# Expert weights stored four rows to a partition, and an earlier transpose of the next expert's rows

## Chip, cores and metric

One NeuronCore of a Trainium2 chip runs the whole program: two decoder layers over 1024 tokens. The metric is the device time in microseconds. Five engines work side by side, each through its own list of instructions in order: TensorE (PE; its weight loads are listed as PEld), VectorE (DVE), ScalarE (ACT), GpSimd (POOL) and SyncE (SP), which issues most of the transfers (DMA) between the chip's memory (DRAM) and the on-chip memory SBUF. TensorE writes its results to PSUM.

## The reference

Each of two layers adds two things to a stream of 1024 tokens by 1024 features: a mixer (eight heads of forgetting attention and eight of latent attention, then an output projection) and a mixture of experts. Only the second matters here. A token is normed, goes to one of 8 groups and to 2 of the 4 experts of its group, and an expert is a gated network of width 256:

```python
group_p = jax.nn.softmax((xt @ w_group).astype(jnp.float32), axis=-1)
group_w, group_id = lax.top_k(group_p, 1)
...
top_logits, local_id = lax.top_k(in_group, TOP_K_IN_GROUP)
gates = group_w * jax.nn.softmax(top_logits, axis=-1)
...
h = jax.nn.silu(xb @ w_gate[e]) * (xb @ w_up[e])
return h @ w_down[e]
...
y = jax.ops.segment_sum(contrib, tok_sorted, num_segments=T)
```

There are 32 experts in each layer. `w_gate` and `w_up` of one are 1024 x 256, `w_down` is 256 x 1024, all float32, 3 MB together. A last norm closes the program.

## The kernel before

**Arithmetic.** A matmul in full precision is done in three passes: each operand is split into a high part (ScalarE copies it into a shorter format, `hi`) and a low part (VectorE subtracts, `lo`), and `mm3` (lines 195 to 197) adds high x high, high x low and low x high. Activations are the stationary operand and the split weights the moving one.

**Experts.** Each expert has room for 96 rows (`RB`). `moe` (line 1541) runs a software pipeline over n = 0 to 32: in step n the current expert is n, the one before is n - 1 and the next is n + 1. All engines but SyncE take their instructions in the order in which the program lists them (`manual_schedule`, line 97). The stages of an expert are functions in `expert` (line 1426):

- `load_a` (1434) and `load_b` (1448): SyncE loads gate and up weights (`load_gu`, line 347, four transfers of 512 KB into two tiles) and down weights (one of 1 MB). Eight tiles hold gate and up weights of four experts; a load waits until the tile it overwrites has been split.
- `gather` (1458): GpSimd clears a tile and fetches the expert's rows from the stored norm `xn_d` by index, three steps ahead.
- `piece(j)` (1465): splits 128 x 1024 weights, on ScalarE (1468) and VectorE (1469). Pieces 0 to 3 are gate and up, each with two of the eight blocks of 128 features; 4 and 5 are down.
- `flip_x` (1473): eight transposes of the gathered rows on TensorE (1479), and a split of each half (185 on ScalarE, 186 on VectorE).
- `gate_up(q)` (1482): twelve matmuls of 512 columns for each half q; `silu` (1491); `flip_h` (1496): two transposes of the product and a split; `down` (1503): twelve matmuls; `result` (1512): two copies on ScalarE (1515, 1516) and a scatter on GpSimd.

**Order of a step.** Engines see, in this order:

```python
cur["gate_up"](0);  pieces_to(6 * n + PC[0])   # PC = (1, 4)
prev["flip_h"]();   cur["gate_up"](1)
prev["down"]();     pieces_to(6 * n + PC[1])
cur["silu"]();      prev["result"]()
nxt["flip_x"]();    pieces_to(6 * n + 6)
```

The pieces of step n are, by `ORDER` (line 53), (n,4), (n,5), (n+1,0), (n+1,1), (n+1,2), (n+1,3): one behind `gate_up(0)`, three behind `down`, two at the end of the step. `gate_up(0)` of an expert reads its pieces 0 and 1, `gate_up(1)` pieces 2 and 3.

**Layout of the weights.** Feature f of the model lies in partition f mod 128 of block f // 128. A gate or up transfer takes 512 rows of 256 floats: from DRAM each run is one row, 1 KB, and in SBUF gate and up alternate within a block, so that a block's 512 columns are gate beside up.

**The norm.** Ahead of the loop the output projection makes the residual tiles; `norm` (1095) squares, scales and stores each in `xn_d` (VectorE at 1103). The last of the eight tiles is done in halves on GpSimd (`norm_half`, 1118, line 1125), and `halves` (1109) splits the first expert's gate and up weights there, with GpSimd in VectorE's place (1113).

Of the kernel before, what the change touches and what calls it, by code (L numbers as in the profile page):

```python
# [20 lines left out]
P = 128  # L21
# [61 lines left out]
def kernel(ctx: ExitStack, tc: tile.TileContext, x, positions, attn_norm, w_in, b_f, q_norm, w_uq,  # L83
# [48 lines left out]
    # gains, one feature per partition  # L132
# [31 lines left out]
    def rsqrt(dst, v, n, tag, c=1.0):  # L164
        """dst = c * v ** -0.5, with a Newton step behind the engine's own power."""
        y = small.tile([P, n], F32, name="rs_y", tag=f"rs_y{tag}")
        pool.tensor_tensor(y, v, mhalf[:, 0:n], op=OP.pow)  # L167
        t = small.tile([P, n], F32, name="rs_t", tag=f"rs_t{tag}")
        pool.tensor_tensor(t, y, y, op=OP.mult)  # L169
        pool.tensor_tensor(t, t, v, op=OP.mult)  # L170
        pool.tensor_scalar(t, t, -0.5 * c, 1.5 * c, op0=OP.mult, op1=OP.add)  # L171
        pool.tensor_tensor(dst, y, t, op=OP.mult)  # L172
# [9 lines left out]
    def split(hi, lo, src, scale=None):  # L182
        """hi + lo = src * scale, each with as many bits as one pass of the tensor engine carries."""
        if scale is None:
            act.activation(hi, src, AF.Copy)  # L185
            dve.tensor_tensor(lo, src, hi.bitcast(F32), op=OP.subtract)  # L186
        else:
            act.activation(hi, src, AF.Copy, scale=scale)
            dve.scalar_tensor_tensor(lo, src, scale, hi.bitcast(F32), op0=OP.mult, op1=OP.subtract)

    def mm3(ps, sh, sl, mh, ml, kcs, first=True, last=True):
        """ps += s.T @ m over the chunks, three passes."""
        n = len(kcs)
        for i, kc in enumerate(kcs):
            pe.matmul(ps, sh(kc), mh(kc), start=first and i == 0, stop=False)  # L195
            pe.matmul(ps, sh(kc), ml(kc), start=False, stop=False)  # L196
            pe.matmul(ps, sl(kc), mh(kc), start=False, stop=last and i == n - 1)  # L197
# [15 lines left out]
    # DRAM kept between phases  # L213
# [5 lines left out]
    def combined(l, i, ht, y_):  # L219
        """The residual stream's tile behind layer l - 1."""  # L220
        if l == 0:
            return ht
        for j in range(2):
            y = y_(j)
            sp.dma_start(y, y_d[l - 1][j * T + i * P:j * T + (i + 1) * P])
            dve.scalar_tensor_tensor(ht, y, gates[:, j, i:i + 1], ht, op0=OP.mult, op1=OP.add)  # L226
        if l < DEPTH:
            sp.dma_start(h_d[2 * l - 1][i], ht)
        return ht
# [106 lines left out]
    def gu_tiles(p, tags=("mix", "mix"), more=None):  # L336
        r = []
        for t in tags:
            q = p
            if t == "mix":  # L340
                gu_n[0] += 1
                if GUX and gu_n[0] > 8 and gu_n[0] % 9 == 0 and more is not None:
                    q, t = more, "gux"
            r.append(q.tile([P, 4, 2 * FF], F32, name="gu", tag=t))
        return r

    def load_gu(raw, wg_, wu_):
        for q in range(2):
            ks = slice(q * 512, q * 512 + 512)
            sp.dma_start(raw[q][:, :, 0:FF], wg_[ks].rearrange("(k p) n -> p k n", p=P))  # L350
            sp.dma_start(raw[q][:, :, FF:], wu_[ks].rearrange("(k p) n -> p k n", p=P))
# [6 lines left out]
    def mixer_open(l):  # L358
        """What a layer can load before the one in front of it is through."""
        # room of the latents, which takes tiles of the residual stream first  # L360
# [17 lines left out]
    def mixer(l, opened):  # L378
        h_in = [xv[i] for i in range(NT)] if l == 0 else h_d[2 * l - 1]
        h_out = h_d[2 * l]  # L380
        # operands of a forgetting head as rows: q_hi twice, q_lo, 1, 1, c_hi, c_lo; k_lo, k_hi, -c_hi, -c_lo, 1, 1
# [123 lines left out]
        # ---- values, queries and keys of the forgetting heads; beside it what hangs on misc -  # L505
# [32 lines left out]
        def forget_a():  # L538
            # log_sigmoid(z) = min(z, 0) - log1p(exp(-|z|)); log1p by its series in u / (2 + u)
            z, u, s1, s2 = t_("fz"), t_("fu"), t_("fs"), t_("fs2")  # L540
            fl.update(z=z, u=u, s1=s1, s2=s2)
            dve.tensor_tensor(z, misc[:, :, 0:H], bft[:, l][:, None, :].to_broadcast([P, NT, H]), op=OP.add)
            dve.scalar_tensor_tensor(u, z, -1.0, z, op0=OP.mult, op1=OP.min)
            act.activation(u, u, AF.Exp)
# [17 lines left out]
        def forget_c():  # L562
            # sums within a token tile, and behind them those of the tiles before
# [82 lines left out]
        def v_scale(g, tp):  # L646
            # a power of two that puts the largest value between 2**14 and 2**15
# [28 lines left out]
        def late_pools():  # L676
            # where the values and misc were: weights of the latent projections, tables of the rotation
# [256 lines left out]
        def fin_a(h):  # L934
            # normed rows: y / sqrt(mean(y * y) + eps * Z * Z), with y and Z scaled alike
# [24 lines left out]
        def fin_c(p, half, bank=1):  # L960
            ysb = pairs[p][0].rearrange("p t s d -> p t (s d)")
            # the bank of the second head's results, which the next pair comes to use later
# [10 lines left out]
        # the output projection's weights, two blocks of rows to a piece, where attention has done  # L973
# [120 lines left out]

        def norm(i):
            ht = hts[i]
            sp.dma_start(h_out[i], ht)
            if i < NT - 1:
# [4 lines left out]
                dve.scalar_tensor_tensor(xn, ht, rs[:, i:i + 1], gb, op0=OP.mult, op1=OP.mult)  # L1103
# [5 lines left out]
        def halves(j):  # L1109
            hi, lo = hl[j]  # L1110
            raw = early[0][j // 2][:, j % 2 * 2:j % 2 * 2 + 2].rearrange("p k n -> p (k n)")
            act.activation(hi, raw, AF.Copy)
            pool.tensor_tensor(lo, raw, hi.bitcast(F32), op=OP.subtract)
# [3 lines left out]
        def norm_half(c):  # L1117
            """What the last tile's norm can do half by half."""
# [6 lines left out]
            pool.tensor_tensor(xn[:, cs], hts[NT - 1][:, cs], gb[:, cs], op=OP.mult)  # L1125
# [4 lines left out]
        # the router's operands are the tile before its norm: w_rt carries the gains, the gates' exponents the scales  # L1130
# [18 lines left out]
        def route_group(rg, a, b, lg=None):  # L1149
            """Experts, gates and ranks of the tokens of tiles a to b, and their entries in the blocks."""  # L1150
# [43 lines left out]
            # ranks within an expert by token; block NT holds the counts  # L1194
# [23 lines left out]
            # gates  # L1218
# [17 lines left out]
        # weights of the first experts, where attention's values and then its results have been  # L1236
        gu_n[0] = 0
        raw0 = v1.tile([P, 2, 4, 2 * FF], F32, name="V", tag="V")
# [11 lines left out]
        for i in range(NT):  # L1250
# [25 lines left out]
            if i == NT - 1:  # L1276
                # the first expert's gate and up weights in two parts, where those of w_o have been
# [35 lines left out]
        # rows of the blocks: which assignment sits where  # L1313
# [10 lines left out]
        # the experts' counts, and the number of further blocks they need  # L1324
# [7 lines left out]
        # behind the rows of the first experts  # L1332
# [13 lines left out]
    def more_tables(l):  # L1346
        """Blocks for the rows of an expert beyond the first RB: their experts, and which assignment sits where."""
# [28 lines left out]
        # of an assignment: the first further block of its expert, the block and the row its rank puts it in  # L1376
# [11 lines left out]
        # block of + qd - 1 where qd > 0, none elsewhere  # L1388
# [20 lines left out]
    def moe_open(l, v0, v1, mp, early, downs, dn_close, hl, hl_close, spare_close):  # L1409
# [16 lines left out]
        def expert(pools, wg_, wu_, wd_, gi, si, n=None):  # L1426
            """The stages of one block of rows, each to be issued where its engines have time."""
# [6 lines left out]
            def load_a():  # L1434
# [5 lines left out]
                e["raw"] = [raw[q][:, k:k + 2] for q in range(2) for k in (0, 2)]  # L1440
# [24 lines left out]
            def piece(j, eng=dve):  # L1465
                hi, lo = hl.popleft()
                raw = (e["raw"][j] if j < 4 else e["rawd"][j - 4]).rearrange("p k n -> p (k n)")
                act.activation(hi, raw, AF.Copy)  # L1468
                eng.tensor_tensor(lo, raw, hi.bitcast(F32), op=OP.subtract)  # L1469
# [12 lines left out]
            def gate_up(q):  # L1482
                if q == 0:
                    e["gu"] = ps_([RB, 2 * FF], F32, name="gu")
                at = lambda w: lambda k: w[k // 2][:, (k % 2) * 512:(k % 2) * 512 + 512]
# [55 lines left out]
    def moe(l, m):  # L1541
# [16 lines left out]
        for n in range(NE + 1):  # L1558
# [10 lines left out]
            if cur:  # L1569
                cur["gate_up"](1)  # L1570
            if prev:
# [6 lines left out]
            if l == DEPTH - 1 and n >= KEPT and len(kept) < NT:  # L1578
                # the weights are through: their room takes the residual stream for the last step
                for raw in gu_tiles(mp):  # L1580
                    for t in range(2):
                        kept.append(raw.rearrange("p k n -> p (k n)")[:, t * D:(t + 1) * D])
                        sp.dma_start(kept[-1], h_d[2 * l][len(kept) - 1])
            if nxt:
                nxt["flip_x"]()
# [103 lines left out]
```

## Time and profile before

| | us |
|---|---|
| median of three runs | 1997.6 |
| lowest and highest | 1996.01, 2002.56 |
| profiled execution, span from first to last instruction | 1997.8 |
| TensorE busy | 1760.9 (88%) |
| VectorE busy | 1347.5 (67%) |
| ScalarE busy | 1187.7 (59%) |
| GpSimd busy | 568.4 (28%) |

The page shows the span alone for the profiled execution and no time around it. It moved 427.11 MB in 243684 DMA packets, 146470 of them of 512 B to under 2 KB. In its slices of 50 us the DMA engines are full in two places, from about 650 to 950 us and from about 1600 to 1940 us: the expert loops of the two layers. A group's line gives the engine's busy time in it, the mean of one instruction, and how long the engine stood idle just before such instructions and whom it waited for. In a window's row the busy times stand in the order PE, PEld, DVE, ACT, POOL; a timeline row gives the start, how long, the engine, the line, output <- input with partitions x elements, how many were merged, and in brackets the idle time before and whom it waited for. A matmul's duration contains its way through the array; matmuls follow each other faster than they last.

### The profile page before, as it was taken

How to read it: one execution, taken by the hardware profiler on the slowest of the kernel's cores; microseconds unless marked ns; L12 is line 12 of the kernel's file. 1: busy time of each engine (PE TensorE's matmuls, PEld its weight loads, DVE VectorE, ACT ScalarE, POOL GpSimd, SP SyncE). 2: the span in 40 equal slices, each digit the busy share in tenths (PEclk: the TensorE clock that was granted, in tenths of full speed). 3: DMA queues.
4: the chain of work that ended last, by engine and by line, in shares of the span. 5: the costliest groups of instructions: out<-in, count | busy, mean ns of one | idle time of the engine just before them, and what ended most of it. 6: DMA issues, size and time to landing. Idle time of an engine off the chain costs nothing. (4 is left out here: it accounts for less than half of the span.)

```text
span 1997.8 us, 33752 instructions
## 1 busy us (share of the span) xinstructions
PE 1760.9 (88%) x12509; PEld 1420.1 (71%) x12509; DVE 1347.5 (67%) x2172; ACT 1187.7 (59%) x2254; POOL 568.4 (28%) x857
## 2 busy tenths in 40 slices
PE   7999899999995999998499997999999689998870
PEld 6987688888883666666399786888888556666650
DVE  6454388887246888877555355888852678887756
ACT  4443278788214888877344235888841278887751
POOL 4001044234114333331230021623330333332305
PEclk9999999999997999999799998999999889999995
DMA  4257833553755999999742775334455499999986
GB/s 157 64 126 218 261 119 108 114 123 96 251 185 180 345 333 333 327 325 331 284 137 54 203 242 183 126 101 109 114 196 209 148 297 324 327 332 322 321 295 235
DMA packets 243684, 427.11 MB, mean 214 GB/s; under 512 B 22166, under 2 KB 168636, under 8 KB 240444
## 3 DMA queue, kind: packets, MB, share of 16 engines
q1 hardware_dynamic: 228092, 387.14, 61.2%
q0 software_dynamic: 14336, 33.58, 5.2%
q10 hardware_dynamic: 1088, 4.19, 0.7%
q8 instruction: 100, 1.64, 0.3%
q14 instruction: 68, 0.56, 0.1%
HBM read 347.24 MB, written 94.37 MB: 221 GB/s over the span
## 5 line engine op out<-in xcount | busy, mean ns | idle before, releaser
L1469 DVE TENSOR_TENSOR lo<-gu,hi 128x1024 fp32r<-128x1024 f32 x248 | 292.6, 1222 | 41.6 <-ACT hi L1468 41.6
L1468 ACT ACTIVATE hi<-gu 128x1024 fp32r<-128x1024 f32 x248 | 248.4, 1054 | 26.4 <-DMA gu<-in_w_up_dram 20.5
L195 PE MATMUL gu<-hi,V 128*96 128x512 f32 x512 | 214.8, 420 | 38.4 <-ACT V L185 38.4
L885 PE MATMUL S<-op 96*128 96x512 f32 (+3 forms) x960 | 228.8, 372 | 20.2 <-DMA op<-FK 13.2
L897 DVE TENSOR_REDUCE nm<-S 128x1 f32<-128x1024 f32 (+7 forms) x256 | 183.2, 752 | 69.3 <-PE S L889 69.3
L906 ACT ACTIVATE pr<-S,nm 128x1024 f32<-128x1024 f32 (+7 forms) x256 | 188.9, 754 | 38.0 <-DVE nm L897 37.9
L197 PE MATMUL gu<-hi,V 128*96 128x512 f32 x512 | 210.0, 410 | 0.0
L196 PE MATMUL gu<-lo,V 128*96 128x512 f32 x512 | 205.7, 402 | 0.0
L916 ACT ACTIVATE ph<-pt 128x512 f16<-128x512 f32 x288 | 157.1, 600 | 66.8 <-PE pt L914 65.8
L917 DVE SCALAR_TENSOR_TENSOR pl<-pt,ph 128x512 f16<-128x512 f32 x288 | 184.7, 682 | 8.6 <-ACT ph L916 7.8
L885 PEld LDWEIGHTS S<-op 96*128 96x128 f32 (+1 forms) x960 | 161.5, 196 | 37.5 <-DMA wor<-in_w_o_dram 14.5
L1517 POOL DMA_INDIRECT y<-V,sidx x64 | 59.7, 932 | 441.6 <-ACT V L1516 417.4
L914 PE MATMUL pt<-ident,pr 128*128 128x128 f32 x1152 | 154.9, 278 | 8.5 <-ACT pr L906 4.8
L1469 DVE TENSOR_TENSOR lo<-dn,hi 128x1024 fp32r<-128x1024 f32 x128 | 155.9, 1219 | 4.2 <-ACT hi L1468 3.9
L1468 ACT ACTIVATE hi<-dn 128x1024 fp32r<-128x1024 f32 x128 | 134.9, 1055 | 4.7 <-DMA dn<-in_w_down_dram 4.7
L195 PEld LDWEIGHTS gu<-hi,V 128*96 128x96 f32 x512 | 84.9, 166 | 74.1 <-ACT V L185 50.3
L914 PEld LDWEIGHTS pt<-ident,pr 128*128 128x128 f32 x1152 | 125.0, 143 | 13.7 <-ACT pr L906 12.9
L928 PE MATMUL y<-V,ph 128*128 128x64 f16 x2304 | 121.7, 193 | 2.8 <-ACT ph L916 1.6
L197 PEld LDWEIGHTS gu<-hi,V 128*96 128x96 f32 x512 | 84.6, 165 | 53.8 <-DVE V L186 21.9
L928 PEld LDWEIGHTS <-ph 128*128 128x128 f16 x2304 | 116.9, 98 | 5.2 <-ACT ph L916 1.8
L928 PE MATMUL y<-V,pl 128*128 128x64 f16 x1152 | 117.1, 193 | 1.1 <-DVE pl L917 1.0
L186 DVE TENSOR_TENSOR V<-pt,V 128x384 fp32r<-128x384 f32 x128 | 65.5, 552 | 69.1 <-ACT V L185 68.9
(363 smaller groups left out, 4318.5 us busy)
## 6 DMA issues: line engine op xcount, KB each, us to landing
gu<-in_w_gate_dram SPq DMA_DIRECT2D x124, 512.0 KB
gu<-in_w_up_dram SPq DMA_DIRECT2D x124, 512.0 KB
dn<-in_w_down_dram SPq DMA_DIRECT2D x60, 1024.0 KB
raw<-in_w_in_dram SPq DMA_DIRECT2D x48, 256.0 KB
h<-ht SPq DMA_DIRECT2D x17, 512.0 KB
FQ<-st SPq DMA_DIRECT2D x32, 256.0 KB
FK<-st SPq DMA_DIRECT2D x32, 256.0 KB
MQ<-st SPq DMA_DIRECT2D x16, 512.0 KB
```

Of the source, the lines that this page charges most:

```text
L195: pe.matmul(ps, sh(kc), mh(kc), start=first and i == 0, stop=False)
L196: pe.matmul(ps, sh(kc), ml(kc), start=False, stop=False)
L197: pe.matmul(ps, sl(kc), mh(kc), start=False, stop=last and i == n - 1)
L885: pe.matmul(o, a[0:k, qs], b[0:k, c0:c0 + n], start=bank not in started, stop=pi == len(passes) - 1 and not diag, skip_group_check=True)
L897: dve.tensor_reduce(nm, u["S"][:, col:col + (qb + 1) * P], axis=AX.X, op=OP.max, negate=True)
L906: act.activation(u["pr"][:, s], u["S"][:, s], AF.Exp, bias=nm, accum_out=zst[h // 2][:, qb, h % 2:h % 2 + 1])
L914: pe.transpose(pt[:, b], u["pr"][:, (4 * q + b) * P:(4 * q + b + 1) * P], ident)
L916: act.activation(u["ph"][:, ks], pt, AF.Copy, scale=P_SCALE)
L917: dve.scalar_tensor_tensor(u["pl"][:, ks], pt, P_SCALE, u["ph"][:, ks], op0=OP.mult, op1=OP.subtract)
L928: pe.matmul(yst[h][:, qb], a[:, b], v[:, kb, h % H, c], start=first_y[h], stop=(kb == qb and s == 2), skip_group_check=True)
L1468: act.activation(hi, raw, AF.Copy)
L1469: eng.tensor_tensor(lo, raw, hi.bitcast(F32), op=OP.subtract)
```

## The change

Gate and up weights are loaded with partition p holding rows 8p to 8p + 7, in two halves of four rows, gate and up apart. The stored norm takes the same order of features: block k, position p holds feature 8p + k, so the norm reads with a step of eight elements. The readers of the weight tiles (splits and matmuls) take gate and up as two blocks. `flip_x` of the next expert is listed behind `gate_up(1)` and ahead of the previous expert's `down`. Comments are removed.

```diff
-            r.append(q.tile([P, 4, 2 * FF], F32, name="gu", tag=t))
+            r.append(q.tile([P, 2, 4, FF], F32, name="gu", tag=t))
...
         for q in range(2):
-            ks = slice(q * 512, q * 512 + 512)
-            sp.dma_start(raw[q][:, :, 0:FF], wg_[ks].rearrange("(k p) n -> p k n", p=P))
-            sp.dma_start(raw[q][:, :, FF:], wu_[ks].rearrange("(k p) n -> p k n", p=P))
+            ks = slice(q * 4, q * 4 + 4)
+            sp.dma_start(raw[q][:, 0], wg_.rearrange("(p k) n -> p k n", k=KC)[:, ks])
+            sp.dma_start(raw[q][:, 1], wu_.rearrange("(p k) n -> p k n", k=KC)[:, ks])
...
+        def by_chunk(t):
+            return t.rearrange("r (p k) -> r k p", k=KC)
+
+        def chunked(t):
+            return t.rearrange("r (k p) -> r k p", k=KC)
...
-                dve.scalar_tensor_tensor(xn, ht, rs[:, i:i + 1], gb, op0=OP.mult, op1=OP.mult)
+                dve.scalar_tensor_tensor(chunked(xn), by_chunk(ht), rs[:, i:i + 1], by_chunk(gb), op0=OP.mult, op1=OP.mult)
...
-            raw = early[0][j // 2][:, j % 2 * 2:j % 2 * 2 + 2].rearrange("p k n -> p (k n)")
+            raw = early[0][j // 2][:, :, j % 2 * 2:j % 2 * 2 + 2].rearrange("p g k n -> p g (k n)")
+            hi, lo = (w.rearrange("p (g n) -> p g n", g=2) for w in (hi, lo))
...
-            pool.tensor_tensor(xn[:, cs], hts[NT - 1][:, cs], gb[:, cs], op=OP.mult)
+            ps_ = slice(c * P // 2, c * P // 2 + P // 2)
+            pool.tensor_tensor(chunked(xn)[:, :, ps_], by_chunk(hts[NT - 1])[:, :, ps_], by_chunk(gb)[:, :, ps_], op=OP.mult)
...
-                e["raw"] = [raw[q][:, k:k + 2] for q in range(2) for k in (0, 2)]
+                e["raw"] = [raw[q][:, :, k:k + 2].rearrange("p g k n -> p g (k n)") for q in range(2) for k in (0, 2)]
...
-                raw = (e["raw"][j] if j < 4 else e["rawd"][j - 4]).rearrange("p k n -> p (k n)")
-                act.activation(hi, raw, AF.Copy)
-                eng.tensor_tensor(lo, raw, hi.bitcast(F32), op=OP.subtract)
+                raw = e["raw"][j] if j < 4 else e["rawd"][j - 4].rearrange("p k (g n) -> p (k g) n", g=2)
+                h_, l_ = (w.rearrange("p (g n) -> p g n", g=2) for w in (hi, lo))
+                act.activation(h_, raw, AF.Copy)
+                eng.tensor_tensor(l_, raw, h_.bitcast(F32), op=OP.subtract)
...
-                at = lambda w: lambda k: w[k // 2][:, (k % 2) * 512:(k % 2) * 512 + 512]
+                at = lambda w: lambda k: w[k // 2].rearrange("p (g k n) -> p g k n", g=2, k=2)[:, :, k % 2]
...
             if cur:
                 cur["gate_up"](1)
+            if nxt:
+                nxt["flip_x"]()
             if prev:
                 prev["down"]()
...
-            if nxt:
-                nxt["flip_x"]()
             pieces_to(6 * n + 6)
```

## Rows read from the trace of the kernel before

**Rows 1.** Windows: us, engines' busy us (count), granted clock, DMA share, GB/s.

```profile
500.00:550.00 50.00, 50.00 (x261) 41.88 (x260) 13.61 (x18) 10.15 (x21) 8.11 (x26) 1.00 0.72 252
...
700.00:750.00 50.00, 48.01 (x234) 33.19 (x233) 42.97 (x51) 41.13 (x61) 16.29 (x15) 1.00 1.04 332
...
850.00:900.00 50.00, 45.25 (x212) 30.92 (x211) 39.58 (x47) 38.81 (x57) 16.39 (x15) 0.97 1.02 326
...
1950.00:2000.00 50.00, 0.00 (x0) 0.00 (x0) 28.56 (x23) 9.20 (x16) 28.37 (x48) 0.50 0.59 217
```

**Rows 2.** Timeline, ScalarE, `silu`: start us, us, engine, line, operation.

```profile
641.70 0.38 ACT L1493 ACTIVATE hs<-gu 96x256 f32<-96x256 f32 x1 [1.94 <-PE gu L197]
...
648.98 0.37 ACT L1493 ACTIVATE hs<-gu 96x256 f32<-96x256 f32 x1
...
857.23 0.36 ACT L1493 ACTIVATE hs<-gu 96x256 f32<-96x256 f32 x1
...
946.02 0.36 ACT L1493 ACTIVATE hs<-gu 96x256 f32<-96x256 f32 x1
...
955.63 0.38 ACT L1493 ACTIVATE hs<-gu 96x256 f32<-96x256 f32 x1 [1.51 <-PE gu L197]
...
1613.89 0.38 ACT L1493 ACTIVATE hs<-gu 96x256 f32<-96x256 f32 x1 [2.40 <-PE gu L197]
...
1930.19 0.38 ACT L1493 ACTIVATE hs<-gu 96x256 f32<-96x256 f32 x1 [1.51 <-PE gu L197]
```

**Rows 3.** Timeline of one expert, all engines.

```profile
701.57 0.86 ACT L185 ACTIVATE V<-pt 128x384 fp32r<-128x384 f32 x2
...
702.08 1.02 DVE L186 TENSOR_TENSOR V<-pt,V 128x384 fp32r<-128x384 f32 x2 [1.12 <-ACT V L185]
...
702.10 0.48 PE L195 MATMUL gu<-hi,V 128*96 128x512 f32 x1 [0.40 <-ACT V L185]
...
702.31 2.01 ACT L1468 ACTIVATE hi<-gu 128x1024 fp32r<-128x1024 f32 x2
...
702.41 0.39 PE L196 MATMUL gu<-lo,V 128*96 128x512 f32 x1
...
703.40 2.36 DVE L1469 TENSOR_TENSOR lo<-gu,hi 128x1024 fp32r<-128x1024 f32 x2 [0.30 <-ACT hi L1468]
...
704.86 0.39 PE L197 MATMUL gu<-hi,V 128*96 128x512 f32 x1
...
705.49 0.39 PE L196 MATMUL gu<-lo,V 128*96 128x512 f32 x1
...
708.02 0.40 PE L195 MATMUL py<-hi,V 128*96 128x512 f32 x1
...
710.57 0.39 PE L197 MATMUL py<-hi,V 128*96 128x512 f32 x1
...
710.80 0.82 PE L1479 MATMUL pt<-ident,x 96*128 96x96 f32 x8
...
711.00 0.59 ACT L1516 ACTIVATE V<-py 96x512 f32<-96x512 f32 x1
```

**Rows 4.** Groups, 700 to 800 us: count | busy us, mean ns | idle.

```profile
L1469 DVE TENSOR_TENSOR lo<-gu,hi 128x1024 fp32r<-128x1024 f32 x41 | 48.4, 1221 | 3.0 <-ACT hi L1468 3.0
...
L1468 ACT ACTIVATE hi<-gu 128x1024 fp32r<-128x1024 f32 x40 | 40.0, 1055 | 0.0
...
L1479 PE MATMUL pt<-ident,V 96*128 96x96 f32 x56 | 5.8, 246 | 0.0
```

**Rows 5.** Timeline, ScalarE, first expert of layer 0.

```profile
642.03 0.88 ACT L185 ACTIVATE V<-pt 128x384 fp32r<-128x384 f32 x2
```

**Rows 6.** GpSimd's timeline; VectorE's groups by shape.

```profile
606.01 1.33 POOL L1125 TENSOR_TENSOR xn<-ht,gb 128x512 f32<-128x512 f32 x1
...
L1203 DVE TENSOR_REDUCE ee<-tmp 128x4 f32<-128x128 f32 x4 | 1.1, 286 | 0.1
...
L1178 DVE TENSOR_REDUCE ing<-tmp 128x16 f32<-128x128 f32 x2 | 0.8, 378 | 0.1
```

More of the change, by code (lines that the diff above doesn't have):

```diff
@@ L1237, in mixer @@
         gu_n[0] = 0
-        raw0 = v1.tile([P, 2, 4, 2 * FF], F32, name="V", tag="V")
+        raw0 = v1.tile([P, 2, 2, 4, FF], F32, name="V", tag="V")
         early = [[raw0[:, 0], raw0[:, 1]]]
@@ L1581, in moe @@
                     for t in range(2):
-                        kept.append(raw.rearrange("p k n -> p (k n)")[:, t * D:(t + 1) * D])
+                        kept.append(raw[:, t].rearrange("p k n -> p (k n)"))
                         sp.dma_start(kept[-1], h_d[2 * l][len(kept) - 1])
-            if nxt:
-                nxt["flip_x"]()
             pieces_to(6 * n + 6)
```

## The prediction

> **What bounds the kernel now.** I read the windows by 50 us first. The change touches the loop over the 32 experts, which runs once in each layer. In a window from the first two thirds of it (700 to 750) [rows 1] TensorE is busy 48.0 of 50 us, VectorE 43.0, ScalarE 41.1, and the DMA engines are full (share 1.04, as queues overlap). Later (850 to 900) [rows 1] the DMA share is the same and TensorE has fallen to 45.25. So two things have to be told apart: what sets the pace while weights lie ready, and from where on weights are late.
>
> The starts of the activation `silu`, one for each expert, answer that. From the second expert to the 23rd of layer 0 they stand 208.25 us apart, 21 intervals of 9.917 us. The next eight take 88.79, or 11.10 each [rows 2]. DMA delivers one expert in about 11.1 us at full share, the engines use one in 9.92, and the four experts loaded ahead are used up after 22. From the first to the last `silu` layer 0 takes 313.93 us and layer 1 316.30 [rows 2]. Without late weights it would be 7.28 + 29 x 9.917 + 9.61 = 304.5. Late weights cost 9.4 and 11.8 us, 21.2 in all, and no change to the loads alone can win more than that.
>
> The 9.92 us are TensorE's. Its matmuls of 512 columns follow each other every 0.232 us (708.02 to 710.57, 11 steps), and its transposes every 0.082 (eight in 0.82, one 0.246), so 36 and 10 of them fill 9.17 us of the 9.92. What is left, 0.75, is the stall behind the transposes of the next expert's rows: 0.40 us until ScalarE has split them, then a step of 0.31 instead of 0.232 behind a matmul that has waited, and a wait for VectorE's part [rows 3, 4]. That is what bringing the transposes forward could win, 0.75 x 30 x 2 = 45 us, if nothing new waited.
>
> **The move of the transposes.** `flip_x` is not eight transposes alone. It is also two ScalarE splits and two VectorE subtractions, and these engines take their instructions in the order of the program. So the splits move up ScalarE's queue too: past `result`'s two copies, `silu` and three weight pieces, (n,5), (n+1,0) and (n+1,1). Until now those pieces ran while TensorE did `gate_up(1)` and `down`. Now they stand behind a split that waits for transposes that stand behind `gate_up(1)`. And the next `gate_up(0)` needs the pieces (n+1,0) and (n+1,1). A circle closes in each expert; I add it up from the start of the first split:
> - two splits, 0.74 (701.57 to 702.31) [rows 3];
> - piece (n,5) on ScalarE, 1.055, and 0.03 until VectorE takes it (702.31 + 1.055 against 703.40) [rows 3, 4];
> - its subtraction: two take 2.36, one 1.221, so the next starts 1.14 behind it; that one is (n+1,0), 1.22, and 0.05 to TensorE (two splits in 0.86, overlapped by 0.1, are 0.48 each, so the first ends at 702.05, and the matmul that needs it starts at 702.10) [rows 3, 4]. So far 4.24;
> - TensorE: the matmul with this low half, which has waited, 0.31; nine more of 0.232, 2.09; from the last of `gate_up(0)` over the two transposes of `flip_h` to the second of `gate_up(1)` 0.63 (704.86 to 705.49); eleven steps, 2.55, to the first transpose of the expert after; the fourth ends three steps of 0.082 and one duration of 0.246 later, 0.49; 0.03 to ScalarE [rows 3, 4]. That is 6.10.
>
> The circle is 4.24 + 6.10 = 10.35 us. A second way round, over `silu` and the copies, is as long: ScalarE overlaps two instructions by 0.1 us (2.01 for two of 1.055), so 0.74 + 3 x 0.955 + 0.27 + 2 x 0.49 = 4.86, then piece (n+1,2), 1.055 + 0.03 + 1.22 + 0.05, to 7.22; the first way reaches the same matmul at 4.24 + 0.31 + 2.09 + 0.63 = 7.27 [rows 2 to 4]. Counted so, the order of before comes out at 9.93, against 9.92 measured. So the 0.75 us stall goes, and a wait of about 1.0 us at the second matmul of `gate_up(0)`, for VectorE's low half of piece 0, takes its place. ScalarE then idles between `flip_h` and the splits.
>
> At the ends of the loop: with no `down` before the first expert, TensorE's order there is unchanged and its first split can still start at 642.03 [rows 5], but `silu` now comes behind it and three pieces: 642.03 + 0.74 + 2.87 = 645.64, 3.94 later than 641.70 [rows 2]. Behind the last expert there is no split, so its `silu` comes 6.4 us behind the one before: TensorE's way from the split, 4.24 + 0.31 + 2.09 + 0.63 + 2.32 + 0.43 = 10.02, less the 3.61 to the `silu` before. A layer takes 3.94 + 30 x 10.35 + 6.41 = 320.85 us, both 641.7, where before took 313.93 + 316.30 = 630.2. **The move costs 11.5 us, if weights are never late.**
>
> The gather of an expert's rows is issued two experts ahead and the buffers free up earlier, so GpSimd's queue has slack. No wait of SyncE depends on the move but the freeing of weight buffers, which follows the pieces.
>
> **The loads.** Each gate and up load falls from 512 runs of 1 KB to 128 of 4 KB, so SyncE's count of instructions stays. What a full share moves is to be seen in windows: 332 GB/s at a share of 1.04 in the loop, 319 for a full share, against 252 at 0.72 (350) beside the output projection and 217 at 0.59 (368) in the last step, where rows of 4 KB move [rows 1]. So between nothing and 15 per cent; I take 10, since the down weights of the loop already move in 4 KB, and 11.1 becomes 10.0. Either way weights are hardly late. With 11.1 kept, the deficit against 10.35 is 30 x 0.75 = 22.5 us, and before lived off its lead for 21 x (11.10 - 9.92) = 24.8 us. So this edit wins the 21.2 us, already counted in the sum above, and nothing beyond; the slower loop alone would have won nearly as much. For TensorE's clock I count nothing: the window with 45.25 us busy was granted 0.97 of 2.4 GHz [rows 1], and its waits came in larger lumps.
>
> **The new views.** ScalarE, VectorE and TensorE read gate and up in two blocks instead of one. No row shows that. The nearest is the same instruction on one block, so 0. At the far end stands the reduction that steps by four elements, 0.378 us for 128 of them against 0.286 in a row [rows 6]: 0.09 for an instruction, four pieces and a subtraction in the second way round, up to 0.4 in an expert.
>
> **The norm** reads every eighth element, so that the rows can be stored in the new order. Seven tiles of a layer do it on VectorE, which is busy 13.6 of 50 us there (500 to 550) [rows 1], at no cost. The last tile's second half is on GpSimd (1.33 us, 606.01) [rows 6], on the way to the gather. Between 0 and 0.33 of 1.33 by the strided reduction, up to 1.0 by its marginal cost; VectorE, which stands still behind GpSimd there, can do part of its work first, so I take 0.5 in each layer, 1 us.
> The Trainium skill (GPSIMD Engine Reference, 7. Performance pitfalls for Q7 kernels) says that GpSimd reading SBUF with steps above 8 bytes pays about half more for an element. By that the step would cost 0.65 in each layer and the sum would be 0.3 us higher; no run here shows it on GpSimd yet, the reduction's 0.378 against 0.286 on VectorE points the same way.
>
> **Sum.** 11.5 + 1 = 12.5 us on a span of 1997.8, which lies 0.2 above the median of the three times: 2010 us.
>
> **Rivals.**
> 1. *Faster: the stall goes and no circle closes.* The loop runs at TensorE's own 9.17 us, and the loads at 10.0 live off the lead (30 x 0.83 = 25 of 24.8 us). A layer takes 304.5 - 22.5 = 282, both 66 less than before: 1932. For it: TensorE's stall is real. Against it: it needs ScalarE to take pieces ahead of a split that stands before them in its queue. 6 in 100.
> 2. *The two cancel.* The circle is 10.2 or less; each 0.1 is 6 us, so 1995 to 2003. For it: the sum has many small terms. Against it: the same terms give before to 0.01. 12 in 100.
> 3. *Slower by more: the two-block views cost up to 0.4 in an expert,* in a circle where every term counts: 2010 + 60 x 0.4 = 2034. It decides from about 0.15 upward (2019). 16 in 100.
> 4. *The loads don't change:* the runs stay at 1 KB. Then the lead just lasts: 2010 to 2012. 4 in 100.
>
> My own forecast, 2003 to 2019, has the remaining 62. A range of 2000 to 2034 leaves out rival 1, part of 2 and what lies above 3. Less than 0.3 per cent, 6 us, can't be told from no change; so slower is 0.79 (forecast, 3 and 4, less a little), same 0.14, faster 0.07.
>
> **What would show it.** `silu` every 10.3 to 10.4 us, evenly to the end of the loop, with no ScalarE wait for gate or up weights. The largest TensorE wait in the loop on VectorE's subtraction of a gate/up piece, at L196, of about 1 us for each expert; ScalarE's largest on the transposes of `flip_x`, some 2 us; none left of TensorE on the split. 64 x 1536 = 98,000 DMA packets fewer, and a DMA share below 1 in the loop. The L1468 instructions still 1.05 us. Intervals of 9.3 us would make me wrong on ScalarE's order, 9.9 or late weights on the loads, and longer pieces would be rival 3.

## The result, and the profile after

The changed kernel takes 2018.3 us (median of 4 runs, 2014.7 to 2019.8); the kernel before takes 1996.8 (4 runs, 1991.1 to 2002.6). The ratio is 1.0095, 95% interval 1.0075 to 1.0116: slower, by about 1%. The forecast was 2010 on a profiled span of 1997.8; the profiled span after is 2018.0, so +20.2 where +12.5 was forecast.

The windows of the kernel after, with the columns of [rows 1]; the last one is the first step of the loop in layer 0:

```profile
500.00:550.00 50.00, 50.00 (x257) 41.72 (x256) 16.66 (x18) 10.17 (x21) 8.27 (x27) 1.00 0.75 254
700.00:750.00 50.00, 45.16 (x224) 31.48 (x223) 41.50 (x50) 38.14 (x59) 18.18 (x15) 1.00 1.01 361
850.00:900.00 50.00, 45.13 (x222) 31.30 (x221) 41.17 (x50) 38.11 (x59) 16.58 (x14) 1.00 0.97 344
900.00:950.00 50.00, 45.36 (x224) 31.43 (x222) 41.45 (x48) 38.14 (x58) 14.79 (x13) 1.00 0.77 269
645.00:652.00 7.00, 5.63 (x13) 3.47 (x14) 6.39 (x7) 6.05 (x7) 0.38 (x1) 0.52 0.82 279
```

Against [rows 1], TensorE's busy time fell from 48.0 to 45.2 of 50 us between 700 and 750, and now it stays there to the end: the loop has one pace. DMA moves 361 GB/s at a share of 1.01, where it moved 332 at 1.04.

The starts of `silu` in the timeline of ScalarE (as [rows 2]): the first two and the last two of layer 0, the first and the last of layer 1:

```profile
647.86 0.38 ACT L1504 ACTIVATE hs<-gu 96x256 f32<-96x256 f32 x1
659.08 0.37 ACT L1504 ACTIVATE hs<-gu 96x256 f32<-96x256 f32 x1
...
959.91 0.37 ACT L1504 ACTIVATE hs<-gu 96x256 f32<-96x256 f32 x1
966.34 0.38 ACT L1504 ACTIVATE hs<-gu 96x256 f32<-96x256 f32 x1 [1.09 <-PE gu L197]
...
1631.01 0.38 ACT L1504 ACTIVATE hs<-gu 96x256 f32<-96x256 f32 x1
...
1949.52 0.38 ACT L1504 ACTIVATE hs<-gu 96x256 f32<-96x256 f32 x1 [1.10 <-PE gu L197]
```

From the second to the 31st there are 29 intervals in 300.83 us, 10.37 each (forecast 10.35), and none is longer because of weights. The last is 6.43 (forecast 6.41). The first is 11.22, for which the sum had 10.35 as well.

One expert's circle in the timeline of all engines (as [rows 3]):

```profile
701.21 0.47 PE L196 MATMUL gu<-lo,V 128*96 128x512 f32 x1 [0.96 <-DVE lo L1480]
...
706.77 0.82 PE L1490 MATMUL pt<-ident,V 96*128 96x96 f32 x8
707.30 0.87 ACT L185 ACTIVATE V<-pt 128x384 fp32r<-128x384 f32 x2 [2.35 <-PE pt L1490]
...
708.05 1.06 ACT L1479 ACTIVATE hi<-dn 128x1024 fp32r<-128x1024 f32 x1
...
709.15 1.23 DVE L1480 TENSOR_TENSOR lo<-dn,hi 128x1024 fp32r<-128x1024 f32 x1 [0.31 <-ACT hi L1479]
...
710.29 2.36 DVE L1480 TENSOR_TENSOR lo<-gu,hi 128x1024 fp32r<-128x1024 f32 x2
...
711.56 0.48 PE L196 MATMUL gu<-lo,V 128*96 128x512 f32 x1 [0.97 <-DVE lo L1480]
```

ScalarE has waited 2.35 us when the transposes come. From its split at 707.30 to the matmul at 711.56 it is 4.26 us (forecast 4.24); from the same matmul one expert earlier, 701.21, to the split it is 6.09 (forecast 6.10). TensorE's wait in front of that matmul, 0.96 and 0.97, stands where the stall in front of L195 stood in [rows 3].

The groups from 700 to 800 us, by shape (as [rows 4]):

```profile
L1480 DVE TENSOR_TENSOR lo<-gu,hi 128x1024 fp32r<-128x1024 f32 x40 | 47.2, 1220 | 2.5 <-ACT hi L1479 2.5
L1479 ACT ACTIVATE hi<-gu 128x1024 fp32r<-128x1024 f32 x39 | 39.2, 1063 | 0.0
L196 PE MATMUL gu<-lo,V 128*96 128x512 f32 x80 | 32.2, 403 | 9.7 <-DVE lo L1480 9.7
...
L185 ACT ACTIVATE V<-pt 128x384 fp32r<-128x384 f32 x18 | 7.9, 489 | 21.4 <-PE pt L1490 21.4
```

The two-block views cost nothing to speak of: 1220 ns against 1221 for the subtraction, 1063 against 1055 for the split. The last column is the whole new loop: 9.7 us of TensorE behind the low half, 21.4 of ScalarE behind the transposes, in some ten experts.

The loads did what they say: the page's DMA line has 98,304 packets fewer than the 243,684 of before, for the same bytes.

```profile
DMA packets 145380, 427.11 MB, mean 212 GB/s; under 512 B 22166, under 2 KB 37564, under 8 KB 142140
```

**Where the 20.2 us are.** I cut the span at the first gate/up matmul of a loop (634.09 and 1605.82 before, 635.18 and 1618.44 after) and its last `silu`. The two loops take 331.16 + 331.08 us instead of 321.54 + 324.37: +16.3. Ahead of the first loop +1.1, between the loops +1.9, behind the second +0.9. These are cuts of one profiled execution of each kernel. Over the eleven kernels that were profiled, the stretch between the loops takes from 647.6 to 652.1 us, with no order by what was changed, so differences of this size outside the loops can't be put down to the change.

### The profile page after: what moved, and what is told of

It is laid out like the page before. It is cut to its first block, busy times and chain, and to the rows that moved or that the text cites. A ratio compares the mean times of both kernels' runs of the same rounds, so it can differ in the third digit from the quotient of the medians.

```text
span 2018.0 us, 33809 instructions
## 1 busy us (share of the span) xinstructions
PE 1753.7 (87%) x12509; PEld 1416.8 (70%) x12509; DVE 1367.5 (68%) x2172; ACT 1174.5 (58%) x2254; POOL 591.9 (29%) x857
## 5 line engine op out<-in xcount | busy, mean ns | idle before, releaser
L1480 DVE TENSOR_TENSOR lo<-gu,hi 128x1024 fp32r<-128x1024 f32 x248 | 292.4, 1221 | 15.8 <-ACT hi L1479 15.8
L196 PE MATMUL gu<-lo,V 128*96 128x512 f32 x512 | 209.2, 409 | 59.5 <-DVE lo L1480 59.5
L1479 ACT ACTIVATE hi<-gu 128x1024 fp32r<-128x1024 f32 x248 | 249.2, 1063 | 0.0
L195 PE MATMUL gu<-hi,V 128*96 128x512 f32 x512 | 208.8, 408 | 5.0 <-ACT hi L1479 5.0
L197 PE MATMUL gu<-hi,V 128*96 128x512 f32 x512 | 204.5, 399 | 0.0
L196 PEld LDWEIGHTS gu<-lo,V 128*96 128x96 f32 x512 | 83.9, 164 | 111.7 <-DVE lo L1480 79.8
L185 ACT ACTIVATE V<-pt 128x384 fp32r<-128x384 f32 x128 | 56.1, 489 | 171.5 <-PE pt L1490 171.2
L1479 ACT ACTIVATE hi<-dn 128x1024 fp32r<-128x1024 f32 x128 | 136.1, 1063 | 0.0
```

The costliest lines, as they stand in the source:

```text
L1479: act.activation(h_, raw, AF.Copy)
L1480: eng.tensor_tensor(l_, raw, h_.bitcast(F32), op=OP.subtract)
```

## The experiments

Nine kernels, each timed beside the kernel before on the same chip (medians of it from 1997.6 to 2000.7 us); a ratio below is to that one, with its 95% interval in brackets. The theory: the order alone costs the time, through the circle over ScalarE's queue; the loads alone win only the late weights. The rivals: the views or the loads cost something; the loop's start, with ScalarE's table load or TensorE's clock, holds what the forecast lacks.

**e1_order_only.** The kernel before, with the transposes moved and nothing else.

```
             if cur:
                 cur["gate_up"](1)
+            if nxt:
+                nxt["flip_x"]()
             if prev:
                 prev["down"]()
...
-            if nxt:
-                nxt["flip_x"]()
             pieces_to(6 * n + 6)
```

> The kernel before with only flip_x moved ahead of down; loads of 1 KB runs, norm and views as before. Theory (the move closes a circle over ScalarE, VectorE and TensorE): silu every 10.37 us as in the changed kernel, and weights hardly late, since 11.1 us for an expert against 10.37 uses 30 x 0.73 = 22 us of a lead of 25; some 17 us slower than before, 2015. Rival (the time lies in the loads or the two-block views): 9.92 us between silus while weights are ready, and about 1998.

Measured: 2017.4 us, ratio 1.0096 (1.0077 to 1.0116). `silu` in ScalarE's timeline, first two and last two of layer 0:

```profile
645.49 0.38 ACT L1493 ACTIVATE hs<-gu 96x256 f32<-96x256 f32 x1
656.58 0.37 ACT L1493 ACTIVATE hs<-gu 96x256 f32<-96x256 f32 x1
...
957.41 0.37 ACT L1493 ACTIVATE hs<-gu 96x256 f32<-96x256 f32 x1
963.86 0.38 ACT L1493 ACTIVATE hs<-gu 96x256 f32<-96x256 f32 x1 [1.09 <-PE gu L197]
```

29 intervals in 300.83 us, the same 10.37 to the hundredth, with one-block views and runs of 1 KB. So the order alone makes the whole loss, the views are free, and in a loop this slow the loads are worth nothing: the lead (the weights that lie loaded ahead) lasts with the old ones too.

**e2_loads_only.** The changed kernel with `flip_x` back in its old place (the edit of e1 backwards).

> The changed kernel with flip_x back behind result; loads of 4 KB runs, strided norm and two-block views stay. Theory: silu every 9.92 us to the end of the loop, no weight late, so the 21.2 us of late weights go and the norm and the last step cost some 3: about 1980. Rival 1 (the loads win nothing by themselves, something else was late): uneven intervals from the 23rd expert on as before, 1998 to 2001. Rival 2 (the views cost): intervals above 9.95.

Measured: 1976.9 us, ratio 0.9886 (0.9864 to 0.9908). `silu` in layer 0, the first two and the last two:

```profile
641.53 0.38 ACT L1504 ACTIVATE hs<-gu 96x256 f32<-96x256 f32 x1 [1.17 <-PE gu L197]
648.83 0.36 ACT L1504 ACTIVATE hs<-gu 96x256 f32<-96x256 f32 x1
...
936.53 0.36 ACT L1504 ACTIVATE hs<-gu 96x256 f32<-96x256 f32 x1
946.13 0.38 ACT L1504 ACTIVATE hs<-gu 96x256 f32<-96x256 f32 x1 [1.49 <-PE gu L197]
```

29 intervals in 287.70 us are 9.92, the pace of [rows 2] before weights were late, now to the end; 304.60 from first to last, where 304.5 was worked out for a layer without late weights. The loads win what was late, and the pace of the old order stays.

**e3_pieces_first.** The changed kernel, with the three pieces ahead of the split in ScalarE's queue: the transposes keep their new place, the circle is opened.

```
                 cur["gate_up"](1)
+            pieces_to(6 * n + PC[1])
             if nxt:
                 nxt["flip_x"]()
             if prev:
                 prev["down"]()
-            pieces_to(6 * n + PC[1])
```

> The changed kernel with the three pieces of pieces_to(6n+4) listed ahead of flip_x, flip_x still ahead of down. Theory: the circle opens, since ScalarE does the pieces while TensorE does gate_up(1); TensorE becomes the pace at 36 x 0.232 + 10 x 0.082 = 9.17 us, the loop of a layer is about 39 us shorter, 2018 - 79 = 1939, or up to 1950 if weights at some 10.1 us for an expert are late at the end. Rival (transposes ahead of down cost time whatever ScalarE does, or the loads bind at once): 10.1 us or more between silus, 2002 or more.

Measured: 1970.2 us, ratio 0.9855 (0.9835 to 0.9876), the fastest of the kernels that do the whole work. `silu` in layer 0, the 2nd, 14th, 15th and 31st:

```profile
651.18 0.38 ACT L1504 ACTIVATE hs<-gu 96x256 f32<-96x256 f32 x1
...
761.02 0.37 ACT L1504 ACTIVATE hs<-gu 96x256 f32<-96x256 f32 x1
770.73 0.38 ACT L1504 ACTIVATE hs<-gu 96x256 f32<-96x256 f32 x1
...
934.27 0.38 ACT L1504 ACTIVATE hs<-gu 96x256 f32<-96x256 f32 x1
```

Twelve intervals of 9.15, TensorE's own 9.17 as the prediction counted it; then, after one of 9.71, 16 of 10.22. The expected time, 1939 to 1950, assumed a lead that lasts longer, and missed by 20 us and more. What is late shows in the waits from 780 to 900 us, where the columns are who waits for whom, us in all, times, longest:

```profile
ACT hi L1479 <- DMA dn<-in_w_down_dram: 25.6, 12, 2.5
```

**e4_one_piece_first.** Only piece (n,5) goes ahead of the split; the other two stay behind `down`.

```
                 cur["gate_up"](1)
+            pieces_to(6 * n + 2)
             if nxt:
                 nxt["flip_x"]()
```

> As the changed kernel, but one of the three pieces, (n,5), ahead of flip_x and two behind it. Theory: the circle loses one piece, ScalarE's 0.955 of the three, and by the same sum closes at 9.42 us: loop about 29 us shorter in each layer, 2018 - 59 = 1959. Rival (it is the split's place ahead of the pieces of the next expert that counts, however many): 10.37 us, 2018; other rival (any piece ahead opens it at once): 9.17 us, 1939.

Measured: 1972.1 us, ratio 0.9873 (0.9853 to 0.9893). Three `silu` of layer 0:

```profile
652.86 0.37 ACT L1504 ACTIVATE hs<-gu 96x256 f32<-96x256 f32 x1
662.26 0.37 ACT L1504 ACTIVATE hs<-gu 96x256 f32<-96x256 f32 x1
671.66 0.37 ACT L1504 ACTIVATE hs<-gu 96x256 f32<-96x256 f32 x1
```

9.40 here, and 9.41 on average over 20 of them in layer 1: one instruction out of the circle takes 0.96 us out of it, the 0.955 at which ScalarE's splits follow each other. That sizes the circle. The time, expected as 1959, missed by 13 us, since from the 21st interval of layer 0 and the 22nd of layer 1 on weights are late, as they are in e3.

**e9_no_down_loads.** e3 without the loads of the down weights from the fifth expert on (the buffers keep what the first four brought, and the later experts use that), so that it moves 368.4 MB instead of 427.1.

```
-                if n is None or n > 1:
+                if n is None or 1 < n < NDN:
```

> The kernel with the three pieces ahead of flip_x, which leaves out the loads of the down weights from the fifth expert on (it uses those of the first four again). Theory (from the 14th expert on that kernel waits for delivery alone, at 10.2 us for an expert): silu every 9.17 us to the end of the loop, 18 intervals of 1.0 us less in each layer, some 36 us less in all, 1934. Rival (something else slows the second half, the gathers and scatters or the buffers): intervals of 10 us stay, 1965 or more.

Measured: 1933.5 us, ratio 0.9678 (0.9648 to 0.9707). The first two and last two `silu` of layer 0:

```profile
644.42 0.38 ACT L1504 ACTIVATE hs<-gu 96x256 f32<-96x256 f32 x1
651.34 0.38 ACT L1504 ACTIVATE hs<-gu 96x256 f32<-96x256 f32 x1
...
916.88 0.38 ACT L1504 ACTIVATE hs<-gu 96x256 f32<-96x256 f32 x1
924.58 0.38 ACT L1504 ACTIVATE hs<-gu 96x256 f32<-96x256 f32 x1 [1.10 <-PE gu L197]
```

29 intervals in 265.54 us: 9.16 to the end, and the time as expected. So what stretches e3 to 10.22 is the delivery of weights (its DMA share is 0.99 from 850 to 900 us). The pace of the prediction's rival 1 is real, it was only tied to the wrong order: with the pieces ahead, TensorE does run at its own pace as long as weights are there.

**e8_pieces_first_old_loads.** The order of e3 on the kernel before, with its runs of 1 KB.

```
                 cur["gate_up"](1)
+            pieces_to(6 * n + PC[1])
+            if nxt:
+                nxt["flip_x"]()
             if prev:
                 prev["down"]()
-            pieces_to(6 * n + PC[1])
...
-            if nxt:
-                nxt["flip_x"]()
```

> The kernel before with flip_x ahead of down and the three pieces ahead of flip_x; 1 KB loads, old views and norm. Theory (the engines could do 9.17 us, the loads deliver in 11.1): intervals of 9.17 until the lead is used up, some 12 experts, then 11 and more; the loop ends hardly earlier than before, 1990 to 1998. Rival (delivery isn't the bound there, 4 KB runs matter little): near 1970 as with the new loads.

Measured: 2010.9 us, ratio 1.0065 (1.0045 to 1.0085), slower than before and outside what I expected. Nine intervals of 9.16 in layer 0, then about 11.0. The same wait as in e3, 780 to 900 us:

```profile
ACT hi L1468 <- DMA dn<-in_w_down_dram: 31.9, 11, 3.3
```

So with the good order the loads are worth some 40 us (2010.9 against 1970.2), with the order of the change nothing. Why e8 ends later than the kernel before stays open in the main: a loop that only waits for delivery should end no later, but from the first gate/up matmul to the last `silu` it takes 327.1 and 328.1 us, 5.6 and 3.7 more than before. One part is to be seen in layer 0: ScalarE stands 3.29 us in front of the first step's split, and SyncE's second reload of gate and up goes out 13.6 us behind the first matmul instead of 12.2, so that load starts 1.4 us later.

**e5_table_early.** The changed kernel, with ScalarE's function table for `silu` loaded ahead of the loop by a one-element Silu.

```
         act.activation(cnt, pr[:, NT], AF.Copy)
+        warm = small.tile([P, 1], F32, name="warm", bufs=1)
+        act.activation(warm, cnt[:, 0:1], AF.Silu)
```

> The changed kernel with one silu of 128 x 1 values ahead of the loop, so that ScalarE loads its table (1.28 us) while it waits for the first rows. Theory (the first step's loss is TensorE's 2.5 us wait for weight pieces and the half clock behind it; the table is beside that): the first silu some 1.3 us earlier, the first interval as much longer, the time the same, 2018. Rival (the table load is on the path): 2.6 us less, 2015.5, first interval still 11.2.

Measured: 2011.7 us, ratio 1.0069 (1.0048 to 1.0091), an interval that overlaps the change's. The loops don't explain the difference: the first `silu` comes 1.30 us sooner behind the first gate/up matmul (11.38 against 12.68), the interval behind it is 12.76 instead of 11.22, and from first matmul to last `silu` it is 331.35 and 330.73 against 331.16 and 331.08. The table load (1.28 us) isn't on TensorE's way. The profiled execution is 4.2 us shorter than the changed kernel's, 1.0 of it ahead of the first loop and 2.8 between the loops, where single executions differ by as much.

**e6_first_step.** The changed kernel; the three pieces go ahead of the split in the first step alone.

```
                 cur["gate_up"](1)
+            if n == 0:
+                pieces_to(PC[1])
             if nxt:
                 nxt["flip_x"]()
```

> The changed kernel with the three pieces ahead of flip_x in the first step of each layer alone, all other steps as in the changed kernel. Theory: TensorE doesn't wait 2.5 us in the first step, its granted clock doesn't fall to half there, and the first transposes of the third expert come 5 to 6 us earlier in each layer; 10.37 us from then on; 2006 to 2008. Rival (the 8 us beyond the forecast lie in the norm and the last step): 2014 or more.

Measured: 2006.3 us, ratio 1.0045 (1.0030 to 1.0061). The loops take 326.13 and 326.93, 9.2 us less than after the change in both together; up to the second `silu` it is 5.0 and 4.1 us less, a little under the 5 to 6 expected. The first interval is 9.40, the others stay at 10.37. The window of the first step:

```profile
645.00:652.00 7.00, 6.27 (x34) 4.42 (x33) 5.43 (x7) 4.64 (x8) 0.00 (x0) 1.00 0.63 203
```

34 matmuls at a granted clock of 1.00, where the changed kernel has 13 at 0.52.

**e7_norm_plain.** e3 with the norm reading and storing in a row again; the transposes take the rows' columns with a step of eight instead, so the weights' new order is kept.

```
-                dve.scalar_tensor_tensor(chunked(xn), by_chunk(ht), rs[:, i:i + 1], by_chunk(gb), op0=OP.mult, op1=OP.mult)
+                dve.scalar_tensor_tensor(xn, ht, rs[:, i:i + 1], gb, op0=OP.mult, op1=OP.mult)
...
-            pool.tensor_tensor(chunked(xn)[:, :, ps_], by_chunk(hts[NT - 1])[:, :, ps_], by_chunk(gb)[:, :, ps_], op=OP.mult)
+            pool.tensor_tensor(xn[:, cs], hts[NT - 1][:, cs], gb[:, cs], op=OP.mult)
...
-                        pe.transpose(pt[:, c], e["x"][:, k * P:(k + 1) * P], ident[0:RB, 0:RB])
+                        pe.transpose(pt[:, c], e["x"].rearrange("r (p k) -> r k p", k=KC)[:, k], ident[0:RB, 0:RB])
```

> The kernel with the three pieces ahead of flip_x and 4 KB loads, but the norm is stored in its old order without steps, and the transposes read each eighth element instead. Theory: the last tile's norm is 0.8 us shorter on GpSimd and 1.1 on VectorE, the gather is issued 1 us earlier in each layer; weight loads of TensorE with a step cost nothing beyond their 0.14 us; 1968 against 1970. Rival (a step costs TensorE more than it spares): transposes above 0.1 us each, 8 x 32 x 2 of them, 1972 and up.

Measured: 1971.3 us, ratio 0.9868 (0.9841 to 0.9895), no different from e3. The gather starts 3.2 us sooner (621.58 against 624.81 us in layer 0), but an expert takes 9.36 us instead of 9.15 while weights lie ready. TensorE's weight loads of these rows, from 660 to 720 us, in e7:

```profile
L1489 PEld LDWEIGHTS pt<-ident,V 96*128 96x128 f32 x32 | 4.2, 203 | 0.5
```

and in e3:

```profile
L1490 PEld LDWEIGHTS pt<-ident,V 96*128 96x128 f32 x32 | 3.1, 140 | 0.6
```

The step has to be paid somewhere: once in the norm, or 0.06 us in the weight load of each transpose, of which 0.21 us in an expert's 9.36 are to be seen. In a loop that ends on delivery neither moves the end.

## Why the prediction was right, and where its size was off

**The circle: right, term for term.** 10.37 against 10.35 us an expert (the terms as they stand add up to 10.34), 4.26 and 6.09 against 4.24 and 6.10, the stall turned into the wait at L196. e1 shows it is the order's alone, e4 takes one of its instructions out and shortens it by that instruction, e3 and e9 open it and find TensorE's 9.16 under it. Its price came out as forecast: 29 x 0.45 us in each layer, less the late weights, which the same loop hides.

**The loads: right.** They win what was late (e2: 9.92 to the end) and nothing beyond in this order (e1 is as slow as the change). The size of delivery was a little off: I took 10.0 us for an expert, e3's second half shows 10.22, against 11.10 before. So one sign that I had named, a DMA share below 1 in the loop, did not come in its first two thirds: 10.22 against 10.37 leaves almost no idle share, and the windows give 1.01 and 0.97.

**The views: right,** nothing. The total alone would not have told: 2018.3 lies at the upper end of my own 2003 to 2019, where rival 3 begins. The pieces at 1.06 us and e1's equal pace rule it out.

**The start of the loop: this failed.** The step was "For TensorE's clock I count nothing". The sum gave the two loops 11.5 us; they cost 16.3. Of the 4.8 that are missing, 58 intervals of 10.37 instead of 10.35 make about 1.4, and the first steps 3.4: from the first gate/up matmul to the second `silu` it takes 23.90 us in layer 0 and 23.73 in layer 1, where 7.61 + 3.94 + 10.35 = 21.90 and 8.07 + 14.29 = 22.36 were forecast. The timeline of that step in layer 0:

```profile
642.84 0.87 ACT L185 ACTIVATE V<-pt 128x384 fp32r<-128x384 f32 x2 [6.13 <-PE pt L1490]
...
645.66 0.74 PE L195 MATMUL gu<-hi,V 128*96 128x512 f32 x1 [2.52 <-ACT hi L1479]
...
646.57 1.28 ACT L1504 ACT_TABLE_LOAD   x1
647.11 0.74 PE L196 MATMUL gu<-lo,V 128*96 128x512 f32 x1 [0.71 <-DVE lo L1480]
647.65 0.63 PE L197 MATMUL gu<-hi,V 128*96 128x512 f32 x1
...
651.49 0.63 PE L197 MATMUL gu<-hi,V 128*96 128x512 f32 x1
...
655.48 0.87 ACT L185 ACTIVATE V<-pt 128x384 fp32r<-128x384 f32 x2 [2.77 <-PE pt L1490]
```

There is no `down` yet to cover the split and the pieces, so TensorE stands 2.52 us, does one matmul and stands 0.71 more; behind that its matmuls follow each other every 0.427 us (647.65 to 651.49, nine steps) instead of 0.232: the granted clock of that window is 0.52, its lower level of 1.2 GHz for nearly all of it, until about 652. From the matmul at 647.11 to the next split at 655.48 it takes 8.37 us, where the circle has 6.10. These 2.27 us, less 0.28 by which the first split comes sooner behind the first matmul than was counted, are the 2.0 that layer 0 lacks. In layer 1 (1628 to 1635) the same way takes 8.31 us; there the loop before also began with some us at the lower level, 0.85 us of which the loop after does not have, and 1.4 are left. The sum had the wait in it, but not what follows it. In the loop behind, a wait of 0.96 us in each expert leaves the clock at 1.00.

That the clock and not the waiting makes these 3.4 us is read from the timeline. The first step of e4 bears it out, where the waits are shorter:

```profile
642.19 0.48 PE L195 MATMUL gu<-hi,V 128*96 128x512 f32 x1 [1.57 <-ACT hi L1479]
643.45 0.47 PE L196 MATMUL gu<-lo,V 128*96 128x512 f32 x1 [0.78 <-DVE lo L1480]
```

The clock is granted at 1.00 there from 640 to 652 us, and the steps behind these waits are 0.23 us. e6 takes away the wait and the lower clock at once, with most of the first `silu`'s delay, and gets 9.2 us back.

**The norm: too low.** I took 0.5 us in a layer. In the groups from 440 to 640 us VectorE's part is, in the kernel before:

```profile
L1103 DVE SCALAR_TENSOR_TENSOR xn<-ht,rs,gb 128x1024 f32<-128x1024 f32 x7 | 9.0, 1283 | 13.0 <-POOL rs L172 13.0
```

and the two kinds of the norm are, in the kernel after:

```profile
L1111 DVE SCALAR_TENSOR_TENSOR xn<-ht,rs,gb 128x1024 f32<-128x1024 f32 x7 | 16.3, 2332 | 13.0 <-POOL rs L172 13.0
...
L1135 POOL TENSOR_TENSOR xn<-ht,gb 128x512 f32<-128x512 f32 x2 | 4.1, 2072 | 6.9 <-DMA xn<-xn 6.9
```

GpSimd's half takes 2.07 us instead of 1.33 [rows 6], and its end and the first gather behind it come 1.3 to 1.4 us later (625.64 against 624.33). Among all runs the gather stands between 621.5 and 624.3 in the four kernels with the plain norm (mean 622.8) and between 623.7 and 625.8 in the seven with the stepped one (mean 625.0), so 1.3 is a size with an error of its own. By the two reductions themselves, 0.378 against 0.286 or 32% more, this instruction would have become 0.43 us longer; it became 0.74 longer. The Trainium skill (GPSIMD Engine Reference, 7. Performance pitfalls for Q7 kernels) had said about half more; the trace agrees and has 56% more, and the rule was nearer than my 0.5.

**The sum.** Of the 7.7 us between +12.5 and +20.2, the clock in the first steps makes 3.4 and the intervals 1.4. The other 2.9 are the 3.9 us outside the loops less the 1.0 counted there for the norm. In layer 0 the norm's 1.3 fits the +1.1 ahead of the loop; that it costs as much in layer 1 isn't shown, since the stretch between the loops varies by more (652.1 us in the change, 648.5 in e6, which has the same code there).

**The rivals.** Rival 1 needed the pieces ahead of the split, and that is e3. Rival 3 would have shown longer pieces, rival 4 the old packets; neither is there. Rival 2 would have needed a circle of 10.2 us or less.

Still open: how long the lead lasts. Before it paid for 24.8 us, and I used that number for e3 and e4, where it was 13 to 16 (12 intervals x 1.07 in e3, 19 x 0.85 in e4); with the gather's and the scatter's traffic and other times at which buffers come free, it isn't a constant. No run varied it by itself.

## What to carry to other kernels

Moving a stage up on one engine moves its evictions up on the others too: list what each queue holds between the old and the new place, and follow the way round until it comes back to the same instruction; here two splits put ahead of three weight pieces cost more than the stall that they removed, and moving one more line (e3) turned a loss of 1% into a gain of 1.4%. When a loop gets faster, work out how long the lead of its loads lasts at the new pace, since from there on delivery sets the time. And look at the first step by itself: what the steady loop hides stands open there, and a long wait can be paid twice, as here: once as 2.52 us of waiting and once as 2 us at the lower clock behind it.

## What the runs showed of the hardware

- A weight load of TensorE with a step of 32 B took 203 ns instead of 140, and transposes followed each other every 0.107 us instead of 0.082 (e7 against e3).
- The same step in two inputs cost VectorE 2.33 us for 128x1024 in the norm, against 1.28 in a row before, and GpSimd 2.07 for 128x512 against 1.26 to 1.33.
- With gate and up in runs of 4 KB the loop moved 361 GB/s at a share of 1.01 (356 at 0.99 in e3), with runs of 1 KB 332 at 1.04 [rows 1]; by the pace of late experts that is 10.22 us against 11.10, 8% less.
- TensorE's granted clock fell to half with a wait of 2.52 us, one matmul and a wait of 0.71 us at the loop's start, and stayed at 1.00 with waits of 1.57 and 0.78 us in the same place (e4) and with 0.96 us of waiting in each 10.37.
